# A hybrid decoder layer on one core: scratch rows padded from 34 to 36, and weight loads moved from SyncE's queue to GpSimd's

## The chip, the cores and the metric

The kernel runs on one core of one Trainium2 chip. The metric is device time in microseconds (us) of one execution. Before the change three runs took 1558.58, 1556.44 and 1551.87 us; their median is 1556.44.

Engines are named as in the profile: PE is TensorE (its weight loads are PEld), DVE is VectorE, ACT is ScalarE, POOL is GpSimd, SP is SyncE. L144 is line 144 of the kernel before. Every engine works through its own instructions in the order in which they stand; semaphores tie the engines together. A transfer is issued from one engine's stream, here nearly always from SP.

## The reference

One layer, float32, 528 rows (16 learned rows and 512 frames), width 1024:

```python
h = h + 0.5 * swiglu(rmsnorm(h, norm_ffn1), ffn1_w_in, ffn1_w_out)
u = rmsnorm(h, norm_mix) * valid
P = u @ w_in                       # attention q|k|v, rwkv r|k|v and three loras, two gates
att = sliding_window_attention(rope(q), rope(k), v, sinks)
rw  = token_shift_lerp(rw, rwkv_mu)
rwo = rwkv7_time_mix(...)          # S = S*w + (S a) b' + v k' per step, y = S r
merged = sigmoid(g_att) * (att @ w_attn_branch) + sigmoid(g_rwkv) * (rwo @ w_rwkv_branch)
h = h + merged @ w_out
h = h + 0.5 * swiglu(rmsnorm(h, norm_ffn2), ffn2_w_in, ffn2_w_out)
return rmsnorm(h, norm_final)
```

The time mixing has 16 heads of 64 channels; its state recurrence runs over the rows, one after another.

## The kernel before

Activations lie transposed, channels on the 128 partitions. Three stretches follow each other: the first feed-forward, the mixer, and the output projection with the second feed-forward.

**Weights.** Every dense product takes its weights in tiles of 128 x 512 float32 (256 KB). `load_w` (L135) loads one into a buffer `raw` from SP's queue (L143), ACT rounds it to float32r, `whi` (L144), and DVE takes the rest, `wlo` (L145). `products` (L153) then issues three matmuls per 128 x 128 block (L155 to L157: hi by hi, hi by lo, lo by hi). There are 3 buffers of `raw` and 4 each of `whi` and `wlo` (`WBUFS`), used in turn: a load has to wait until the tile three before it is split, and a split until PE has used the tile four before it.

**The mixer** (`mixer`, L353) is made of generators, one per stage, that a planner interleaves by a table of start times and spans (`PLAN`, `SHIFT`, `LATE`; `run`, L1020); the tile framework's scheduler then fixes each engine's order from its own priorities. The projections, attention (`attend`), gates and the two branch products fill PE around the recurrence.

The recurrence is cut into 8 chunks of 64 rows and a leading part of 16, and the 16 heads into 8 pairs. For pair j the stages are a1 (projections, decay), p (chunk matrices), i (inverse), b (the serial pass over chunks) and t (normalisation, gate). Stage i needs the inverse of unit triangular matrices. For each of the pair's two heads and each chunk it is done by blocks of 32 x 32, through DRAM:

- stage p stores the diagonal blocks into a scratch tensor `Ls` of 34 rows of 32 x 32 (L824, L825): per head 9 upper blocks (8 chunks and the leading part) and 8 lower ones;
- stage i loads `Ls` three times, one copy per column group, to 3 x 34 = 102 partitions of `LT` (L865), and start values to `X` (L866);
- 31 steps of two DVE operations each substitute (L870, `xtmp<-LT,X`; L872, `X<-X,xtmp`);
- three stores bring `X` to a second scratch tensor `Xs` (L876), each 34 rows of 11 pieces of 128 bytes, and four loads bring the blocks from there into `xt` in 32-row transfers (L881, L882);
- `assemble` (L888) adds the off-diagonal block (L894 to L911).

Stage b begins with `pn<-W,g` (L928) and needs `xt` for the first time in `pn<-zy,xt` (L936); DVE and ACT return its result as `W` (L937, L938), PE multiplies again (L941, `py<-W,g`), DVE forms the next `W` (L945, L947).

**POOL** has no transfers. In the mixer it clears buffers: `tm` (L436), `tsx` (L697, L698), `g` (L773), `kbt` (L779), `g1e` and `g1o` (L785), `W` (L833), `LT` (L878). In the feed-forwards it multiplies `sg` (L285).

Of the kernel before, what the change touches and what calls it, by code (L numbers as in the profile page):

```python
# [8 lines left out]
F32 = mybir.dt.float32  # L9
# [4 lines left out]
OP = mybir.AluOpType  # L14
# [94 lines left out]
def hybrid_layer(ctx: ExitStack, tc: tile.TileContext, a, phases="all"):  # L109
    nc = tc.nc  # L110
# [21 lines left out]
    def half(ap):  # L132
        return ap.rearrange("p (h t) -> p h t", h=2)

    def load_w(src, n, M=P, eng=None, pool=None):  # L135

        if pool:
            hi, lo = (pool.tile([P, KW, P], F32R, name=x)[:, :n, :M] for x in ("whi", "wlo"))
        else:
            hi = wp.tile([P, KW, P], F32R, name="whi", bufs=WBUFS[1])[:, :n, :M]  # L140
            lo = wp.tile([P, KW, P], F32R, name="wlo", bufs=WBUFS[2])[:, :n, :M]
        raw = wp.tile([P, KW, P], F32, name="raw", bufs=WBUFS[0])[:, :n, :M]
        nc.sync.dma_start(out=raw, in_=src)  # L143
        nc.scalar.copy(out=hi, in_=raw)  # L144
        (eng or nc.vector).tensor_tensor(out=lo, in0=raw, in1=hi.bitcast(F32), op=OP.subtract)  # L145
        return hi, lo
# [175 lines left out]
    def rsqrt(pool, x, n, eps, cap=3e38, tag="n", scale=1.0):  # L322


        y = pool.tile([P, 16], F32, name=tag + "y")[:, :n]
        t = pool.tile([P, 16], F32, name=tag + "t")[:, :n]
        if eps:
            xs = pool.tile([P, 16], F32, name=tag + "x")[:, :n]
            nc.vector.tensor_scalar(out=xs, in0=x, scalar1=eps, scalar2=None, op0=OP.add)
            x = xs  # L330
        nc.vector.tensor_scalar(out=y.bitcast(I32), in0=x.bitcast(I32), scalar1=-0.5, scalar2=1597463007.0, op0=OP.mult, op1=OP.add)
        for c in (-3.0, -12.0, -768.0):
            nc.vector.tensor_mul(out=t, in0=y, in1=x)  # L333
            nc.vector.tensor_mul(out=t, in0=t, in1=y)  # L334
            nc.vector.scalar_tensor_tensor(out=y, in0=t, scalar=c, in1=y, op0=OP.add, op1=OP.mult)  # L335
        nc.vector.tensor_scalar(out=y, in0=y, scalar1=-scale / 8192, scalar2=cap, op0=OP.mult, op1=OP.min)
        return y
# [15 lines left out]
    def mixer(nm):  # L353
        uh, ul, rstd = nm.sh, nm.sl, nm.rstd
        un.close()
        es = ctx.enter_context(ExitStack())
        ring = es.enter_context(tc.tile_pool(name="mx_r", bufs=2))
        cp = es.enter_context(tc.tile_pool(name="mx_c", bufs=1))
        tp = es.enter_context(tc.tile_pool(name="mx_t", bufs=1))
        sp = es.enter_context(tc.tile_pool(name="mx_s", bufs=2))  # L360
        ap = es.enter_context(tc.tile_pool(name="mx_a", bufs=2))
        ps = es.enter_context(tc.tile_pool(name="mx_ps", bufs=2, space=PSUM))
        dsc = es.enter_context(tc.tile_pool(name="mx_d", bufs=2, space=bass.MemoryType.DRAM))

        def bank(tag):
            if tag in SMALL:
                return small[:, SMALL[tag]]
            return ps.tile([P, 512], F32, name="p" + tag, tag=tag, bufs=BANKS[tag])
# [294 lines left out]
        def pause(n):  # L663
            for _ in range(PAUSE[n]):
                yield

        def chunks(x):
            return x.rearrange("p (c t) -> p c t", t=CH)
# [99 lines left out]
        def stage_p(j, G):  # L768
# [32 lines left out]
            def masked(dst, src, q):  # L801
                m = tri[slice(0, P) if dst.shape[0] == P else LO, q, :]
                if len(dst.shape) == 3:
                    m = m.unsqueeze(1).to_broadcast(list(dst.shape))
                nc.vector.tensor_mul(out=dst, in0=src, in1=m)

            G.Ls = dsc.tile([34, 32, 32], F32, name="Ls")
            for h, U, Vr in ((0, LO, HI), (1, HI, LO)):
                g1, Z, Y = G.g1[h], U, Vr
                pt = bank("s")  # L810
                nc.tensor.matmul(pt[:, 0:P], KBT[:, 0, :], G.g0[:, h, :], start=True, stop=True)
                masked(G.g2[U, 0, :], pt[U, Z], 0)
                masked(G.g0[Vr, h, Z], pt[Vr, Z], 0)
                for c0 in (1, 5):
                    pt = bank("s")
                    for i in range(4):
                        nc.tensor.matmul(pt[:, P * i:P * i + P], KBT[:, c0 + i, :], g1[:, c0 - 1 + i, :], start=True, stop=True)
                    pv = pt.rearrange("p (c t) -> p c t", c=4)
                    masked(G.g2[U, c0:c0 + 4, :], pv[U, :, Z], 0)
                    masked(g1[Vr, c0 - 1:c0 + 3, Z], pv[Vr, :, Z], 0)  # L820
                    masked(g3[:, c0 - 1:c0 + 3, 1 + h, :], pv[:, :, Y], 1)
                    yield
                u = 64 * h
                nc.sync.dma_start(out=G.Ls[17 * h:17 * h + 9].rearrange("c s t -> s c t"), in_=G.g2[u:u + 32, :, 0:32])  # L824
                nc.sync.dma_start(out=G.Ls[17 * h + 9:17 * h + 17].rearrange("c s t -> s c t"), in_=G.g2[u + 32:u + 64, 1:, 32:64])  # L825
            yield
            pb = bank("s")
            nc.tensor.matmul(pb, C("bones"), rkk, start=True, stop=True)
# [27 lines left out]

        def stage_i(j, G):

            Xs = dsc.tile([34, 33, 32], F32, name="Xs")
            G.LT = sp.tile([P, 32, 32], F32, name="LT", bufs=1)  # L860
            LT = G.LT[:102]
            X = sp.tile([102, 11, 32], F32, name="X", bufs=1)
            tmp = sp.tile([102, 11, 32], F32, name="xtmp", bufs=1)
            for q in range(3):
                nc.sync.dma_start(out=LT[34 * q:34 * q + 34], in_=G.Ls)  # L865
            nc.sync.dma_start(out=X, in_=a["xinit"])  # L866
            yield
            for c in range(31):
                n, w = c // 3 + 1, 31 - c
                nc.vector.tensor_tensor(out=tmp[:, :n, :w], in0=LT[:, c:c + 1, c + 1:32].to_broadcast([102, n, w]),  # L870
                                        in1=X[:, :n, c:c + 1].to_broadcast([102, n, w]), op=OP.mult)
                nc.vector.tensor_add(out=X[:, :n, c + 1:32], in0=X[:, :n, c + 1:32], in1=tmp[:, :n, :w])  # L872
                if c % 8 == 7:
                    yield
            for q in range(3):
                nc.sync.dma_start(out=Xs[:, q:33:3, :], in_=X[34 * q:34 * q + 34])  # L876
            G.xt = XT[j % 2]
            nc.gpsimd.memset(G.LT[:, :24, :], 0.0)  # L878
            for h in range(2):
                u, m = 64 * h, 17 * h  # L880
                nc.sync.dma_start(out=G.xt[u:u + 32, :, u:u + 32], in_=Xs[m:m + 9, 0:32, :].rearrange("c s t -> s c t"))  # L881
                nc.sync.dma_start(out=G.xt[u + 32:u + 64, 1:, u + 32:u + 64],  # L882
                                  in_=Xs[m + 9:m + 17, 0:32, :].rearrange("c s t -> s c t"))
            yield
            yield from pause("inv")
            yield from assemble(G)

        def assemble(G):  # L888


            x11, w1 = G.LT[:, :16].rearrange("p (c h) x -> p c h x", h=2), G.LT[:, 16:24]
            for h in range(2):
# [61 lines left out]
        def stage_t(j, G):  # L954
# [4 lines left out]
            spread = lambda x: x.unsqueeze(2).to_broadcast([P, 8, CH])  # L959
            nc.vector.tensor_reduce(out=s1, in_=yg, op=OP.add, axis=AX.X)  # L960
            nc.vector.tensor_scalar(out=s1, in0=s1, scalar1=-1.0 / CH, scalar2=None, op0=OP.mult)
# [3 lines left out]
            nc.scalar.activation(out=sq, in_=ys, func=AF.Square)  # L965
            nc.vector.tensor_reduce(out=s2, in_=chunks(sq), op=OP.add, axis=AX.X)
            rv = rsqrt(sp, s2, 8, CH * GN_EPS, tag="g", scale=8.0)
# [83 lines left out]
        G = [Ctx() for _ in range(NJ)]  # L1051
# [27 lines left out]
        add("rwkv_branch", 0, rwkv_branch(), last, move, g[0])  # L1079
        run(tasks)  # L1080
        assert next(att, None) is None and next(gate, None) is None
        es.close()

    nc.scalar.dma_start(out=vec, in_=a["vec"])
    with ExitStack() as es:
        hp = es.enter_context(tc.tile_pool(name="hp", bufs=1))
        h = hp.tile([P, KD, NT], F32, name="h")
# [30 lines left out]
    with ExitStack() as es:  # L1118
        hp = es.enter_context(tc.tile_pool(name="hp3", bufs=1))
        up2 = es.enter_context(tc.tile_pool(name="up2", bufs=1))  # L1120
        h = hp.tile([P, KD, SEQ], F32, name="h")
# [25 lines left out]
def constants():  # L1147
    c = np.zeros((P, NCON), np.float32)

    def put(n, x):  # L1150
        c[:x.shape[0], CON[n]:CON[n] + x.shape[1]] = x
    put("ident", np.eye(P, dtype=np.float32))
    i = np.arange(P)[:, None] % CH
    jj = np.arange(192)[None, :]
    win = np.where((jj > i) & (jj <= 128 + i), 0.0, 8 * NEG).astype(np.float32)
    z = np.zeros((P, NMETA), np.float32)
    put("am", np.concatenate([win, z], 1))
    b = (np.arange(P)[:, None] // CH == np.arange(P)[None, :] // CH).astype(np.float32)
    put("bones", b)
    x = np.zeros((102, 11, 32), np.float32)  # L1160
    for gcol in range(3):
        for ii in range(11):
            if 3 * ii + gcol < 32:
                x[34 * gcol:34 * gcol + 34, ii, 3 * ii + gcol] = 1
    return c, x


# [61 lines left out]
```

## Time and profile before

The profiled execution took 1557.82 us; the span from its first to its last instruction is 1556.1 us.

| engine | busy in the span, us | share |
|---|---|---|
| PE | 1500.3 | 96% |
| DVE | 900.1 | 58% |
| ACT | 652.9 | 42% |
| POOL | 93.6 | 6% |

| transfers | |
|---|---|
| issued | nearly all from SP (137568 of 137838 packets on its queue) |
| moved | 163.23 MB, mean 105 GB/s |
| weight loads in the mixer | 133 after the norm (`win` 99, `wgd` 2, `wa` 16, `wr` 16) |

Busy shares are means over unlike stretches. Views by stretch, the waits of each engine (who waited for whom, total, times, longest) and the timeline say more. A matmul's end is modelled, so PE counts as busy even where it runs at half clock; the granted clock has a column of its own. A wait is shown with the work that ended last before it was over.

### The profile page before, as it was taken

How to read it: one execution, taken by the hardware profiler on the slowest of the kernel's cores; microseconds unless marked ns; L12 is line 12 of the kernel's file. 1: busy time of each engine (PE TensorE's matmuls, PEld its weight loads, DVE VectorE, ACT ScalarE, POOL GpSimd, SP SyncE). 2: the span in 40 equal slices, each digit the busy share in tenths (PEclk: the TensorE clock that was granted, in tenths of full speed). 3: DMA queues.
4: the chain of work that ended last, by engine and by line, in shares of the span. 5: the costliest groups of instructions: out<-in, count | busy, mean ns of one | idle time of the engine just before them, and what ended most of it. 6: DMA issues, size and time to landing. Idle time of an engine off the chain costs nothing. (4 is left out here: it accounts for less than half of the span.)

```text
span 1556.1 us, 25641 instructions
## 1 busy us (share of the span) xinstructions
PE 1500.3 (96%) x9365; PEld 1325.2 (85%) x9365; DVE 900.1 (58%) x2471; ACT 652.9 (42%) x1468; POOL 93.6 (6%) x153
## 2 busy tenths in 40 slices
PE   9999999999999999998999999999999999999997
PEld 9999999999887888887878887677777888888886
DVE  6334334344764886887978888675655444443334
ACT  5333333233442457465664754635343333332231
POOL 0111111000100000000000000000000111110000
PEclk9999999999999999999989999999999999999998
DMA  5333333344243333323332232555633333333332
GB/s 165 89 93 91 89 93 88 110 120 116 78 121 96 112 84 89 81 81 104 99 98 76 82 101 85 153 183 173 221 95 89 95 95 96 97 97 91 95 97 79
DMA packets 137838, 163.23 MB, mean 105 GB/s; under 512 B 56960, under 2 KB 68288, under 8 KB 137712
## 3 DMA queue, kind: packets, MB, share of 16 engines
q1 hardware_dynamic: 137568, 161.54, 35.4%
q8 instruction: 73, 1.20, 0.3%
q14 instruction: 53, 0.43, 0.1%
q10 hardware_dynamic: 144, 0.06, 0.0%
HBM read 140.03 MB, written 21.52 MB: 104 GB/s over the span
## 5 line engine op out<-in xcount | busy, mean ns | idle before, releaser
L144 ACT CAST whi<-raw 128x512 fp32r<-128x512 f32 (+1 forms) x426 | 258.8, 611 | 576.6 <-PE dn L156 446.5
L145 DVE TENSOR_TENSOR wlo<-raw,whi 128x512 fp32r<-128x512 f32 (+1 forms) x426 | 287.9, 679 | 304.1 <-ACT whi L144 300.0
L155 PE MATMUL dn<-uh,whi 128*128 128x264 f32 (+1 forms) x1320 | 426.8, 323 | 1.9 <-DVE tgt L657 0.9
L156 PE MATMUL dn<-ul,whi 128*128 128x264 f32 (+1 forms) x1320 | 427.3, 324 | 0.3 <-DVE ul L203 0.3
L157 PE MATMUL dn<-uh,wlo 128*128 128x264 f32 (+1 forms) x1320 | 425.0, 322 | 0.0
L155 PEld LDWEIGHTS dn<-uh,whi 128*128 128x128 f32 x1320 | 247.8, 188 | 23.9 <-ACT whi L144 3.2
L157 PEld LDWEIGHTS dn<-uh,wlo 128*128 128x128 f32 x1320 | 248.4, 188 | 19.9
L156 PEld LDWEIGHTS dn<-ul,whi 128*128 128x128 f32 x1320 | 248.4, 188 | 19.0 <-DVE ul L203 0.5
L155 PE MATMUL pdn<-uh,whi 128*128 128x264 f32 (+3 forms) x656 | 229.0, 350 | 4.6 <-ACT whi L144 2.5
L157 PE MATMUL pdn<-uh,wlo 128*128 128x264 f32 (+3 forms) x656 | 224.3, 343 | 3.7 <-DVE wlo L145 3.6
L156 PE MATMUL pdn<-ul,whi 128*128 128x264 f32 (+3 forms) x656 | 224.5, 343 | 0.9 <-DVE ul L253 0.8
L155 PEld LDWEIGHTS pdn<-uh,whi 128*128 128x128 f32 x656 | 127.1, 194 | 17.0 <-ACT whi L144 4.2
L157 PEld LDWEIGHTS pdn<-uh,wlo 128*128 128x128 f32 x656 | 127.0, 194 | 11.4 <-DVE wlo L145 5.0
L156 PEld LDWEIGHTS pdn<-ul,whi 128*128 128x128 f32 x656 | 126.7, 193 | 7.7 <-DVE ul L253 1.7
L155 PE MATMUL dn<-mh,whi 128*128 128x264 f32 (+2 forms) x350 | 110.7, 316 | 0.0
L156 PE MATMUL dn<-ml,whi 128*128 128x264 f32 (+2 forms) x350 | 110.6, 316 | 0.0
L157 PE MATMUL dn<-mh,wlo 128*128 128x264 f32 (+2 forms) x350 | 110.5, 316 | 0.0
L285 POOL TENSOR_TENSOR sg<-sg,rstd 128x528 f32<-128x528 f32 (+1 forms) x44 | 58.0, 1319 | 595.8 <-ACT sg L284 428.9
L286 DVE TENSOR_TENSOR m<-sg,dn 128x528 f32<-128x528 f32 (+1 forms) x44 | 30.6, 696 | 70.9 <-PE dn L157 67.6
L155 PEld LDWEIGHTS dn<-mh,whi 128*128 128x128 f32 x350 | 66.1, 189 | 4.4
L156 PEld LDWEIGHTS dn<-ml,whi 128*128 128x128 f32 x350 | 66.1, 189 | 4.3
L157 PEld LDWEIGHTS dn<-mh,wlo 128*128 128x128 f32 x350 | 66.0, 189 | 4.3
(395 smaller groups left out, 2058.2 us busy)
## 6 DMA issues: line engine op xcount, KB each, us to landing
raw<-win SPq DMA_DIRECT2D x104, 256.0 KB
raw<-w1in SPq DMA_DIRECT2D x88, 256.0 KB
raw<-w2in SPq DMA_DIRECT2D x88, 256.0 KB
raw<-w1out SPq DMA_DIRECT2D x40, 256.0 KB
raw<-w2out SPq DMA_DIRECT2D x40, 256.0 KB
gD<-tgt SPq DMA_DIRECT2D x24, 256.0 KB
raw<-wa SPq DMA_DIRECT2D x16, 256.0 KB
tgt<-gD SPq DMA_DIRECT2D x16, 256.0 KB
```

The source lines that it names most:

```text
L144: nc.scalar.copy(out=hi, in_=raw)
L145: (eng or nc.vector).tensor_tensor(out=lo, in0=raw, in1=hi.bitcast(F32), op=OP.subtract)
L155: nc.tensor.matmul(o, hi, xh[k][:, c], start=(k == 0), stop=False)
L156: nc.tensor.matmul(o, hi, xl[k][:, c], start=False, stop=False)
L157: nc.tensor.matmul(o, lo, xh[k][:, c], start=False, stop=last)
L285: nc.gpsimd.tensor_mul(out=sg, in0=sg, in1=nm.rstd[:, :n])
L286: nc.vector.tensor_mul(out=vw(m), in0=vw(sg), in1=vu)
```

## The change

Two edits.

1. The scratch tensors `Ls` and `Xs` get 36 rows in place of 34, 18 per head, and `X`, `xtmp` and `LT` 3 x 36 = 108 partitions in place of 102. The lower blocks' store now takes all 9 parts, the leading one too, so that each head has 9 + 9 rows; the load of the lower blocks skips that one. The 31 substitution steps are the same, on 108 partitions.
2. `load_w` issues from `queue["w"]`, which is SP's queue in the feed-forwards and the output projection, and POOL's from the mixer's start to its end. The copies to `whi` and `wlo` stay on ACT and DVE.

```diff
+    queue = {"w": nc.sync}
+
     def load_w(src, n, M=P, eng=None, pool=None):
...
-        nc.sync.dma_start(out=raw, in_=src)
+        queue["w"].dma_start(out=raw, in_=src)
...
         es = ctx.enter_context(ExitStack())
+        queue["w"] = nc.gpsimd
         ring = es.enter_context(tc.tile_pool(name="mx_r", bufs=2))
...
-            G.Ls = dsc.tile([34, 32, 32], F32, name="Ls")
+            G.Ls = dsc.tile([36, 32, 32], F32, name="Ls")
...
-                nc.sync.dma_start(out=G.Ls[17 * h:17 * h + 9].rearrange("c s t -> s c t"), in_=G.g2[u:u + 32, :, 0:32])
-                nc.sync.dma_start(out=G.Ls[17 * h + 9:17 * h + 17].rearrange("c s t -> s c t"), in_=G.g2[u + 32:u + 64, 1:, 32:64])
+                nc.sync.dma_start(out=G.Ls[18 * h:18 * h + 9].rearrange("c s t -> s c t"), in_=G.g2[u:u + 32, :, 0:32])
+                nc.sync.dma_start(out=G.Ls[18 * h + 9:18 * h + 18].rearrange("c s t -> s c t"), in_=G.g2[u + 32:u + 64, :, 32:64])
...
             for q in range(3):
-                nc.sync.dma_start(out=LT[34 * q:34 * q + 34], in_=G.Ls)
+                nc.sync.dma_start(out=LT[36 * q:36 * q + 36], in_=G.Ls)
...
             for q in range(3):
-                nc.sync.dma_start(out=Xs[:, q:33:3, :], in_=X[34 * q:34 * q + 34])
+                nc.sync.dma_start(out=Xs[:, q:33:3, :], in_=X[36 * q:36 * q + 36])
...
-                u, m = 64 * h, 17 * h
+                u, m = 64 * h, 18 * h
...
-                                  in_=Xs[m + 9:m + 17, 0:32, :].rearrange("c s t -> s c t"))
+                                  in_=Xs[m + 10:m + 18, 0:32, :].rearrange("c s t -> s c t"))
...
+        queue["w"] = nc.sync
         es.close()
```

The scheduler lays out every engine's order anew. In the changed kernel line numbers are 2 to 5 higher (L143 becomes L145, L876 becomes L880, L936 becomes L940).

SP around the last pair's three stores of `X` and the four loads of `xt`, before:

```order
L1014 DMA pT<-rD 128x512
L643 DMA gD<-tgt 128x512
L143 DMA raw<-wa 128x512
L876 DMA Xs<-X 374x1x32 x3
L643 DMA gD<-tgt 128x512
L637 DMA tgt<-gD 128x512
L143 DMA raw<-wa 128x512
L881 DMA xt_4609<-Xs 32x9x32
```

And in the changed kernel:

```order
L1018 DMA pT<-rD 128x512
L984 DMA tgs<-bD 128x512
L880 DMA Xs<-X 396x1x32 x3
L1018 DMA pT<-rD 128x512 x2
L646 DMA gD<-tgt 128x512
L885 DMA xt_4609<-Xs 32x9x32
```

The weight tiles (`raw<-wa`) are gone from SP; other transfers of 256 KB still stand between the stores and the loads.

POOL around the clearing of `g` for the fourth pair (`g_8031`), before:

```order
L436 MEMSET tm 128x1 x2
L785 MEMSET g1e 64x1024
L785 MEMSET g1o 64x1024
L833 MEMSET W 128x128
L878 MEMSET LT 128x768
L773 MEMSET g_8031 128x256
L436 MEMSET tm 128x1 x2
```

And in the changed kernel:

```order
L439 MEMSET tm 128x1
L145 DMA raw<-win 128x512 x2
L439 MEMSET tm 128x1
L788 MEMSET g1e 64x1024
L788 MEMSET g1o 64x1024
L837 MEMSET W 128x128
L882 MEMSET LT 128x768
L145 DMA raw<-win 128x512
L776 MEMSET g_8031 128x256
L145 DMA raw<-win 128x512 x3
L439 MEMSET tm 128x1
```

The memsets keep nearly their order, and the loads stand between them, singly or up to some ten in a row.

PE at the last pair's first use of `xt`, before:

```order
L155 MATMUL pdn<-uh,whi 128x512
L156 MATMUL pdn<-ul,whi 128x512
L157 MATMUL pdn<-uh,wlo 128x512
L936 MATMUL pn<-zy,xt_4609 128x128
L155 MATMUL pdn<-uh,whi 128x512
L898 MATMUL pt<-LT,gg_11398 128x128 x4
```

And in the changed kernel:

```order
L157 MATMUL pdn<-uh,whi 128x512
L158 MATMUL pdn<-ul,whi 128x512
L159 MATMUL pdn<-uh,wlo 128x512
L940 MATMUL pn<-zy,xt_4609 128x128
L902 MATMUL pt<-LT,gg_11398 128x128 x4
```

Both stand behind dense products of 512 columns. Before, this matmul comes 102 rows after the pair's first W product (`pn<-W,g_11394`), in the changed kernel 54 rows after it.

More of the change, by code (lines that the diff above doesn't have):

```diff
@@ L857, in stage_i @@
         def stage_i(j, G):
-            Xs = dsc.tile([34, 33, 32], F32, name="Xs")
+            Xs = dsc.tile([36, 33, 32], F32, name="Xs")
             G.LT = sp.tile([P, 32, 32], F32, name="LT", bufs=1)
-            LT = G.LT[:102]
-            X = sp.tile([102, 11, 32], F32, name="X", bufs=1)
-            tmp = sp.tile([102, 11, 32], F32, name="xtmp", bufs=1)
+            LT = G.LT[:108]
+            X = sp.tile([108, 11, 32], F32, name="X", bufs=1)
+            tmp = sp.tile([108, 11, 32], F32, name="xtmp", bufs=1)
             for q in range(3):
-                nc.sync.dma_start(out=LT[34 * q:34 * q + 34], in_=G.Ls)
+                nc.sync.dma_start(out=LT[36 * q:36 * q + 36], in_=G.Ls)
             nc.sync.dma_start(out=X, in_=a["xinit"])
@@ L869, in stage_i @@
                 n, w = c // 3 + 1, 31 - c
-                nc.vector.tensor_tensor(out=tmp[:, :n, :w], in0=LT[:, c:c + 1, c + 1:32].to_broadcast([102, n, w]),
-                                        in1=X[:, :n, c:c + 1].to_broadcast([102, n, w]), op=OP.mult)
+                nc.vector.tensor_tensor(out=tmp[:, :n, :w], in0=LT[:, c:c + 1, c + 1:32].to_broadcast([108, n, w]),
+                                        in1=X[:, :n, c:c + 1].to_broadcast([108, n, w]), op=OP.mult)
                 nc.vector.tensor_add(out=X[:, :n, c + 1:32], in0=X[:, :n, c + 1:32], in1=tmp[:, :n, :w])
@@ L1159, in constants @@
     put("bones", b)
-    x = np.zeros((102, 11, 32), np.float32)
+    x = np.zeros((108, 11, 32), np.float32)
     for gcol in range(3):
@@ L1163, in constants @@
             if 3 * ii + gcol < 32:
-                x[34 * gcol:34 * gcol + 34, ii, 3 * ii + gcol] = 1
+                x[36 * gcol:36 * gcol + 36, ii, 3 * ii + gcol] = 1
     return c, x
```

## The prediction

> **What bounds the kernel now.** I read the table of stages first. Its columns are the stretch and its length in us, then the busy time (and the instructions) of PE, PEld, DVE, ACT and POOL, the granted TensorE clock, the DMA share and GB/s.
>
> ```profile
> 0.00:382.00 382.00, 380.31 (x3082) 378.18 (x3083) 162.15 (x252) 132.72 (x215) 30.00 (x28) 1.00 0.36 106
> 382.00:1114.00 732.00, 689.72 (x4340) 593.13 (x4339) 547.33 (x1897) 380.12 (x1026) 34.98 (x103) 0.97 0.37 109
> 1114.00:1556.00 442.00, 430.29 (x1947) 353.84 (x1945) 190.62 (x324) 140.03 (x228) 28.59 (x22) 0.99 0.33 98
> ```
>
> The change acts only in the middle stretch, the mixer (the first weight load that it moves is at 382 us, the last at 1113). TensorE sets the end there too, but it leaves 732.0 - 689.7 = 42.3 us idle and its clock averages 0.97. DVE is busy for 547 of 732 us, POOL for 35. So the ceiling of any gain is the 42 us and the lost clock. The waits of PE in that stretch (total, times, longest) say who owns the idle time:
>
> ```profile
> PE py L941 <- DVE W L937: 5.4, 6, 2.2
> PE pn L928 <- DVE W L947: 5.2, 3, 2.7
> PE pn L936 <- DMA xt<-Xs: 4.7, 4, 2.8
> PE pdn L157 <- DVE wlo L145: 3.6, 3, 2.2
> PE ps L811 <- DVE kbt L794: 2.8, 1, 2.8
> PE pdn L155 <- ACT whi L144: 2.5, 4, 1.1
> ```
>
> The first two are the recurrence, which the change does not touch. The third is the inverse coming back from DRAM. The fourth and sixth are weight tiles that are not split yet, 6.1 us in all. The fifth will turn out to be a transfer as well.
>
> **The padded rows: what they remove.** One pair, the last one, followed through SP, DVE and PE (start, length, instruction; the bracket is idle time and its releaser):
>
> ```profile
> 1039.00 0.17 DVE L872 TENSOR_TENSOR X<-X,xtmp 102x11 f32<-102x11 f32 x1
> ...
> 1039.20 4.70 SPq L876 DMA_DIRECT2D Xs<-X  x3
> 1044.00 2.04 SPq L643 DMA_DIRECT2D gD<-tgt  x1
> ...
> 1048.04 0.33 SPq L881 DMA_DIRECT2D xt<-Xs  x1
> ...
> 1049.41 0.46 SPq L882 DMA_DIRECT2D xt<-Xs  x1
> ...
> 1050.96 0.46 PE L936 MATMUL pn<-zy,xt 128*128 128x128 f32 x2 [2.79 <-DMA xt<-Xs]
> ```
>
> The substitution ends at 1039.17. Its three stores need 4.70 us to issue, and their bytes are there at 1048.04, when the loads that wait for them go out: 8.9 us. Those loads move 2 x 32 x (9 + 8) = 1088 pieces of 128 bytes in 32-row transfers, nearly as many as the stores (3 x 374 = 1122), and PE has them 1050.96 - 1048.04 = 2.9 us after the first is issued. The view of the DMA engines for the first pair's store (583.0 to 589.0 us in 40 slices, tenths busy, then GB/s) says why:
>
> ```profile
> DMA  0000111111111111121222212222211221222212
> GB/s 5 0 0 13 27 27 27 26 27 27 27 27 27 27 26 21 23 22 20 22 22 22 22 20 21 22 22 21 22 20 21 23 22 20 22 22 22 22 20 21
> ```
>
> For over five microseconds one to two tenths of the 16 engines run, about two of them, at 20 to 27 GB/s, and nothing else on SP's queue moves beside them. A 34-row transfer uses about two engines. The first pair's substitution also waits for its input, three 34-row loads:
>
> ```profile
> 531.94 0.91 SPq L865 DMA_DIRECT2D LT<-Ls  x3
> ...
> 543.96 0.19 DVE L870 TENSOR_TENSOR xtmp<-LT,X 102x31 f32<-102x31 f32 x1 [2.57 <-DMA LT<-Ls]
> ...
> 545.02 0.46 PE L811 MATMUL ps<-g,kbt 128*128 128x128 f32 x2 [2.81 <-DVE kbt L794]
> ```
>
> DVE, in order, stands 2.57 us for a load issued 12 us earlier, and PE stands 2.81 us for a product queued behind it. Each of these two stalls costs a second time, in granted clock (the third figure from the right):
>
> ```profile
> 545.00:553.00 8.00, 7.97 (x41) 7.70 (x42) 6.50 (x34) 4.55 (x17) 0.10 (x1) 0.59 0.11 37
> ...
> 1051.00:1058.00 7.00, 6.28 (x22) 5.40 (x23) 2.72 (x7) 2.54 (x8) 0.00 (x0) 0.55 0.66 219
> ```
>
> 8 x 0.41 = 3.3 us and 7 x 0.45 = 3.2 us of PE's time are lost.
>
> The cost of a 36-row transfer is in no row. Bounds: as now (no gain), or as the 32-row loads, 2.9 us instead of 8.9. I take the second end: 36 is the nearest to 32 in rows and pieces. That is 6 us off each store, and more than the 2.57 off the load. The extra work is small: X grows from 374 to 396 pieces, and the DVE steps run over partitions, 108 in place of 102, at the same length.
>
> The Trainium skill, "DMA: Bandwidth & Descriptors", section "Why a DMA increments its semaphore by 16 and not by 1", has a rule for this: a transfer is spread over the largest number up to 16 that divides its slowest dimension, so 34 rows go to 2 engines and 36 to 12. The two tenths above agree for 34; for 36 no run here shows it yet. By that rule the store would take a sixth of its time, some 1 us as an estimate, and the sum below would be the same, since 2.9 us already clears the waits.
>
> Terms. (a) The stall at 545 goes with its clock loss: -2.8 - 3.3 = -6.1. (b) Three smaller waits for xt: 4.7 - 2.8 = -1.9. (c) The stall at 1051 with its clock loss is 2.8 + 3.2 = 6.0, but the new order puts that pair's first use of xt closer behind the pair's start (54 rows of PE after its first W product; 102 before), which uses up part of what the faster store gives. I take half: -3.0. Bounds for (a) to (c): 0 and -14.0.
>
> **The weights on POOL's queue.** 133 loads leave SP (99 + 2 + 16 + 16). What they do now (issue time min/median/max in ns, first and last start; then what the split of a tile waited for, us and times):
>
> ```profile
> L143 SPq DMA_DIRECT2D raw<-win x99: 327/351/846, 387.4 to 985.8; - x99
> L143 SPq DMA_DIRECT2D raw<-wa x16: 332/390/1312, 996.4 to 1052.5; - x16
> L143 SPq DMA_DIRECT2D raw<-wr x16: 327/332/430, 1057.7 to 1113.4; - x16
> L143 SPq DMA_DIRECT2D raw<-wgd x2: 374/378/381, 382.1 to 385.0; - x2
> ...
>   PE pdn L156: 40.6, 37
>   DMA raw<-win: 25.7, 12
> ...
>   DMA raw<-wr: 3.9, 1
>   DMA raw<-wa: 2.6, 3
> ```
>
> An issue takes SP 0.35 us. The ACT cast of a tile waits 37 times for PE to release a buffer (the load was early) and 16 times for the load, 32.2 us in all; of these PE sees the 6.1 us above. Part of the lateness is SP's order, for a load stands behind transfers that wait:
>
> ```profile
> SPq L613 <- ACT ao L611: 28.3, 11, 5.2
> SPq L737 <- ACT rw L735: 27.6, 7, 11.2
> SPq L998 <- DVE tys L996: 24.1, 4, 11.7
> ```
>
> Away from SP a load no longer waits for ao, rw or tys, nor behind two busy engines. (d) I take a third of the 6.1 us: -2.0; bounds 0 and -6.1. On POOL it instead stands behind memsets, which wait too (longest groups of POOL; busy, mean ns of one | idle before):
>
> ```profile
> L785 POOL MEMSET g1e<- 64x1024 f32 x8 | 7.6, 952 | 53.5 <-PE pn L928 53.4
> L436 POOL MEMSET tm<- 128x1 f32 (+1 forms) x27 | 2.6, 98 | 321.4 <-DVE tr L446 177.6 <-DVE tk L446 63.8 <-DVE tv L446 49.4
> ```
>
> Most of that idle time is POOL arriving early with nothing else to do, and the scheduler has put the loads between memsets of about the same age. Behind a load that waits for its raw buffer now stand the memsets, for which DVE and PE wait; the tm memset is 98 ns of work and its wait was DVE's own.
>
> What POOL needs to issue a load is in no row. Bounds: SP's 0.35 us below; above, POOL's own largest operation:
>
> ```profile
> L285 POOL TENSOR_TENSOR sg<-sg,rstd 128x528 f32<-128x528 f32 (+1 forms) x44 | 58.0, 1319 | 595.8 <-ACT sg L284 428.9
> ```
>
> I take the upper, 1.3 us, the one whole-tile operation of POOL that the trace shows. 133 x 1.3 = 173 us of POOL's 732: not a bound. A load lands 1.3 - 0.35 = 1.0 us later. (e) Early loads hide that behind PE's buffers; the 16 late ones do not: 16 us more for ACT, of which PE sees the present share, 6.1 / 32.2 = 0.19: +3.0. Without that cover all 16 us would reach PE. Bounds 0 and +16.
>
> A rule that speaks against the move: the Trainium skill, "SBUF — State Buffer", section "Who interferes with whom", says that a load issued from GpSimd has its descriptors written by GpSimd's cores, which certain DVE operations lock out, and "A bandwidth-pool intuition that's wrong (but worth ruling out)" on the same page gives some 620 ns alone and 3100 ns beside such an operation. No run here shows it; rival 4 works out in rows what it would do.
>
> Sum: -6.1 - 1.9 - 3.0 - 2.0 + 3.0 = -10.0 us. The profiled execution took 1557.82 us (span 1556.1 and 1.7 around it), so 1547.8; the median of the runs shown, 1556.44, is 1.4 lower, which gives **1546.4 us**. By itself this case runs from 1540 to 1552 (a sum of -16 to -4: (c) whole or not at all, (d) and (e) at half or twice what is taken).
>
> **Rivals.** (1) *More comes free.* With SP empty of weights every small transfer of the chain goes out when it is ready, and all of (a) to (d) fall with no cost on POOL: -14.0 - 6.1 = -20.1, thus 1536. For: SP's waits of 80 us in the three rows above. Against: PE sees little of them.
> (2) *Nothing on balance.* The chain is shorter, but DVE, at 547 of 732 us and in order, hands the time on to the recurrence (10.6 us in the first two waits of PE), or the 36-row transfers still use two engines, so that the change does not do what it says: 1554 to 1559.
> (3) *Slower: head of line on POOL.* A load stands behind the g1e memset, which waits for PE to finish with a pair two back (53.4 us over the eight). From the point where that delay exceeds what three raw buffers hold, PE runs dry and the clock drops with it. A stall like the one at 545 costs 2.8 + 3.3 = 6.1 us; in four of the eight pairs that is +24, less the 9 of the padding: +15, thus 1571. For: the memset's waits are long, and POOL cannot reorder. Against: casts find their load early 37 times to 16.
> (4) *Each load held up on POOL by DVE.* DVE is busy three quarters of the stretch; if an issue takes POOL 3 us, still under the 732 / 133 = 5.5 us that it may, the 16 late loads land 2.65 us later, 42 us on ACT, of which PE sees 0.19: +8.0 in place of +3.0, so 1551.4. This is the rule of the SBUF page above.
>
> **How the numbers follow.** What a measurement of this kernel can tell from no change is about 0.5%, 7.8 us: faster is under 1548.7, slower over 1564.2. Forecast 0.38 (0.30 of it faster, 0.08 the same); rival 1 0.17, all faster; rival 2 0.17 (0.13 the same, 0.04 slower); rival 3 0.20 (0.19 slower, 0.01 the same); rival 4 0.08 (0.03 faster, 0.05 the same). Together faster 0.50, same 0.27, slower 0.23. The range takes in rival 1 with some 6 us of the remaining idle time, and rival 3 to its middle: 1530 to 1570.
>
> **What would show it.** Right: the DMA share in a store rises well above two tenths, SP issues the three stores in under 3 us, the waits of PE for xt and for kbt go and the half-clock stretches behind them; waits of ACT for raw stay near 32 us. Wrong: POOL's loads start late behind L785 or L436, PE's waits for whi and wlo grow past 15 us, or the waits for W grow by what xt lost. A mean clock under 0.97 in the mixer would say that new stalls took the place of the old.

## The result and the profile after

The changed kernel takes 1527.62 us (median of four runs, 1526.39 to 1531.18) against 1555.19 us before (four runs: the three above and one of 1553.94): a ratio of 0.983, 95% interval [0.980, 0.985], 27.6 us faster. The forecast was 1546.4 and its range ended at 1530: the sign was right, the size was not, and the sum of the terms (-10.0) held little more than a third of the gain.

The stages of the changed kernel, in the columns of the prediction's first table (busy time by engine, granted clock, DMA share, GB/s):

```profile
0.00:382.00 382.00, 380.17 (x3082) 378.12 (x3083) 162.35 (x252) 132.82 (x215) 29.99 (x28) 1.00 0.36 106
382.00:1087.00 705.00, 678.63 (x4338) 582.57 (x4337) 550.48 (x1899) 381.18 (x1026) 106.74 (x236) 0.98 0.39 115
1087.00:1529.00 442.00, 430.58 (x1948) 354.04 (x1947) 190.19 (x322) 140.43 (x228) 28.61 (x22) 0.99 0.33 96
```

All of it is in the mixer: 705 us in place of 732, the other two stretches are as they were. PE's idle time there fell from 42.3 to 705.0 - 678.6 = 26.4 us; the other 11 us are busy time, which shrank as the granted clock rose from 0.97 to 0.98. POOL's 72 us more are the issuing of loads. The longest waits of PE in that stretch (total, times, longest):

```profile
PE pn L940 <- ACT zy L933: 3.0, 6, 0.8
PE pdn L157 <- DVE tgt L645: 2.5, 1, 2.5
PE pdn L159 <- DVE wlo L147: 2.5, 2, 2.2
PE pt L912 <- ACT LT L906: 2.0, 4, 0.8
```

The waits for `xt` (4.7) and `kbt` (2.8) are gone, and so are most of those for `W` (1.9 us left of 10.6), which the prediction took to lie outside the change. The transfers themselves became faster. SP's timeline at the first pair's store, before and then after (start, length of the issue):

```profile
582.15 4.28 SPq L876 DMA_DIRECT2D Xs<-X  x3
...
590.54 0.33 SPq L881 DMA_DIRECT2D xt<-Xs  x1
```

```profile
579.57 2.58 SPq L880 DMA_DIRECT2D Xs<-X  x3
...
584.32 0.33 SPq L885 DMA_DIRECT2D xt<-Xs  x1
```

From the store's issue to the first load of `xt` it is 4.8 us in place of 8.4. The view of the DMA engines over that store and the loads behind it (580 to 586 us, tenths busy) shows up to nine tenths where it was one or two. Part of it is POOL's: 46% of the 16 engines' time is SP's queue, 23% the weight loads.

```profile
DMA  9998620486130698899968994768998505646445
```

The weight loads on POOL (issue min/median/max in ns), their time to landing, and the waits of ACT's casts for them:

```profile
L145 POOL DMA_DIRECT2D raw<-win x99: 539/539/557, 387.7 to 932.7; - x99
...
DMA to landing us min/median/max: 2.5/3.2/5.7
```

```profile
ACT whi L146 <- PE pdn L158: 88.6, 67, 4.5
...
ACT whi L146 <- DMA raw<-win: 5.7, 3, 3.4
```

An issue costs POOL 0.54 us, the same with DVE busy for 550 of 705 us, and the casts wait 5.7 us for loads in place of 32.2. So both edits do what they say. Which of them carries the gain is a question for the experiments.

### The profile page after: what moved, and what is told of

Same layout as the page of the kernel before. It is cut to its first block, busy times and chain, and to the rows that moved or that the text cites. A ratio compares the mean times of both kernels' runs of the same rounds, so it can differ in the third digit from the quotient of the medians.

```text
span 1529.5 us, 25746 instructions
## 1 busy us (share of the span) xinstructions
PE 1489.4 (97%) x9365; PEld 1314.7 (86%) x9365; DVE 903.0 (59%) x2471; ACT 654.4 (43%) x1468; POOL 165.3 (11%) x286
## 5 line engine op out<-in xcount | busy, mean ns | idle before, releaser
L145 POOL DMA_DIRECT2D raw<-win x99 | 53.4, 539 | 313.7 <-DVE wlo L147 127.4
```

The costliest lines, as they stand in the source:

```text
L145: queue["w"].dma_start(out=raw, in_=src)
```

## The pairs in a row

The traces of all kernels agree in one thing that the prediction did not look at: the distance from one pair to the next. The loads of `LT` (three per pair; issue times in ns, first and last start), before and then after:

```profile
L865 SPq DMA_DIRECT2D LT<-Ls x24: 251/272/324, 531.9 to 989.2; - x24
```

```profile
L869 SPq DMA_DIRECT2D LT<-Ls x24: 306/358/758, 532.6 to 962.6; - x24
```

The first pair starts at the same time; the eighth starts 26.6 us earlier. The seven distances between pairs shrank from 457.3 / 7 = 65.3 to 430.0 / 7 = 61.4 us, 27.3 us together, as much as the gain. One tile keeps the inverse of a pair from overlapping with that of the next: `LT` has one buffer, and `assemble` keeps its last operand in it. In the kernel before, SP's own waits between 420 and 1000 us have this row:

```profile
SPq L865 <- PE pt L908: 10.8, 5, 3.5
```

Five of the seven following loads wait for the last product of `assemble`. So load, 31 steps, store, `xt`, `assemble` and the next load form a loop, and what a transfer loses in it can be lost in every pair, whether PE shows a wait for it or not. How much of it is lost, the runs below have to show. In the table below the four pieces are means over seven pairs, from the start times in the timeline (first `LT` load, first step, first `Xs` store, first `xt` load, next `LT` load); the distance is worked out as above.

| kernel | time, us | distance | load to step | steps | store to xt | xt to next load |
|---|---|---|---|---|---|---|
| before | 1555.2 | 65.3 | 11.3 | 36.6 | 8.5 | 8.8 |
| after | 1527.6 | 61.4 | 8.9 | 35.3 | 5.1 | 12.0 |
| e1 padding alone | 1523.0 | 61.3 | 9.5 | 34.8 | 4.8 | 12.2 |
| e2 queue alone | 1592.9 | 70.1 | 12.2 | 36.9 | 9.0 | 11.9 |
| e3 38 rows, POOL | 1605.8 | 71.3 | 13.1 | 36.7 | 9.9 | 11.6 |
| e4 loads later on POOL | 1533.2 | 62.3 | 8.7 | 36.5 | 5.2 | 11.7 |
| e5 38 rows, SP | 1585.0 | 68.2 | 12.5 | 35.6 | 9.3 | 10.8 |
| e6 40 rows, SP | 1527.9 | 61.5 | 9.2 | 34.1 | 4.9 | 13.2 |
| e7 only the load wide | 1550.0 | 63.3 | 9.8 | 35.4 | 8.8 | 9.2 |
| e8 only the store wide | 1579.0 | 69.2 | 15.1 | 38.0 | 6.3 | 9.6 |
| e9 before, LT free earlier | 1551.5 | 64.3 | 11.8 | 35.3 | 8.4 | 8.8 |
| e10 e1, LT free earlier | 1522.0 | 59.8 | 9.6 | 35.1 | 4.6 | 10.4 |
| e11 before, LT held longer | 1584.1 | 70.3 | 11.2 | 36.5 | 8.4 | 14.0 |
| e12 queue alone, on ACT | 1582.5 | 68.3 | 11.9 | 36.8 | 9.2 | 10.3 |

A straight line through the 14 rows, time against seven distances, has a slope of 1.03 us per us and misses none by more than about 9 us. That by itself is arithmetic more than a cause, since the seven distances are part of the time. It says where the time goes; what makes a distance long is what the runs had to show.

## The experiments

The scheduler lays out every engine anew for each kernel, so single results carry some scatter of order: e1 and e6, two kernels with wide transfers (spread over many DMA engines) and their loads on SP, lie 5 us apart, and e8 below shows that an order can cost far more. All are compared with the kernel before on the same chip.

**One edit at a time (e1, e2).** The first takes the diff of the change with the queue left on SP; the second the queue with 34 rows.

```diff
-        queue["w"] = nc.gpsimd
+        queue["w"] = nc.sync
```

> The padded rows alone; all weights stay on SP's queue. Theory P (the transfers over two engines were nearly the whole cost): 20 us or more below the kernel before, DVE's waits for LT and xt (19 us together before) under 5 us, three Xs stores issued in under 3 us. Theory Q (the in-order queue on SP was the larger part): about the terms (a) to (c) of the prediction, 8 to 12 us below, with ACT's waits for raw still near 30 us.

> The queue alone; 34 rows stay. Theory P: within 5 us of the kernel before, since the stalls at LT and xt remain. Theory Q: 12 to 20 us below, ACT's waits for raw under 10 us, while DVE's waits for LT and xt stay near 19 us. Should both edits alone give their full size, the two add up to the 27.6 us of the change; if they share a cause, they overlap.

The padding alone: 1522.96 us, 0.979 [0.978, 0.981], 32 us faster. The queue alone: 1592.94 us, 1.025 [1.022, 1.028], 38 us slower. The padding is more than the whole gain; the queue edit costs. So the theory that puts the gain on the padding (P) stands, and the one that puts it on the queue (Q) falls. With 36 rows it costs 1527.6 - 1523.0 = 4.7 us, at the edge of what the two intervals tell apart; with 34 rows it costs 38. The edits do not add. In the two profiles as much lies behind the last pair's `LT` load: from there to the end of the mixer it is 119.7 us at a clock of 1.00 with the padding alone, 124.4 at 0.96 with both edits.

DVE's waits for the two transfers, before and with the queue alone:

```profile
DVE xtmp L870 <- DMA LT<-Ls: 10.8, 5, 2.8
DVE LT L894 <- DMA xt<-Xs: 8.2, 7, 1.7
```

```profile
DVE xtmp L873 <- DMA LT<-Ls: 28.8, 7, 5.4
DVE LT L897 <- DMA xt<-Xs: 23.4, 8, 6.5
```

and PE's waits with the queue alone:

```profile
PE pn L931 <- DVE W L950: 14.0, 4, 4.4
PE pn L939 <- DMA xt<-Xs: 13.5, 6, 5.7
PE py L944 <- DVE W L940: 10.4, 5, 4.8
```

DVE stands 52 us in order where it stood 19, and what is queued behind it is the recurrence's `W`. Weight tiles are not what is late here: ACT's waits for `raw` fell, from 32.2 to 20.6 us.

**The number of rows (e3, e5, e6).** 38 rows with the loads on POOL; 38 and 40 rows with the loads on SP. The added rows are filled by one small extra store per pair, and nothing uses them.

```diff
-            G.Ls = dsc.tile([36, 32, 32], F32, name="Ls")
+            G.Ls = dsc.tile([38, 32, 32], F32, name="Ls")
...
+            nc.sync.dma_start(out=G.Ls[36:38].rearrange("c s t -> s c t"), in_=G.g2[0:32, 0:2, 0:32])
```

> The changed kernel with 38 rows in place of 36 (19 x 2; two rows more are filled by one small transfer per pair and used by nothing). If what counts is the number of engines, 38 rows go back to two: the store shows one to two tenths of DMA share for some 6 us again, the three issues take over 4 us, and the time comes out near that of the queue edit alone. If padding helps in another way (row pitch, size), it stays within 4 us of the changed kernel.

> 38 scratch rows, all loads on SP; one small extra transfer per pair fills the two extra rows, which nothing uses. Theory E (the padding pays because 36 rows are spread over many engines): 38 rows are back on two engines, so the three Xs stores take 9 to 11 us until xt can be loaded, PE's waits for xt return and the time is 1553 to 1568, near the 1555 of before. It also repeats the measurement of the queue edit on two-engine rows with another order of instructions: against the 1605.8 of 38 rows with the loads on POOL. Theory O (the padding pays because the scheduler happened to find a better order of instructions, whatever the engines): no relation to the count of engines; the time stays within 10 us of the 1523.0 of 36 rows as likely as not.

> 40 scratch rows, all loads on SP; one small extra transfer per pair fills the four extra rows, which nothing uses. Theory E: the transfer is spread wide again (8 engines if the count is the largest one that divides the rows), so Xs to xt takes 4.5 to 5.5 us and the time is 1522 to 1532, close to the 1523.0 of 36 rows although there are more rows than in the slow 38. Theory O: anything between 1520 and 1570.

Measured: 1605.81 us (1.033 [1.030, 1.035]) for 38 rows on POOL, 1584.97 (1.019 [1.017, 1.022]) for 38 on SP, 1527.88 (0.983 [0.981, 0.984]) for 40 on SP. More rows than 36 are fast at 40 and slow at 38, and store to `xt` goes with it: 4.8, 4.9 us against 9.3, 9.9. That is the rule of the Trainium skill, "DMA: Bandwidth & Descriptors", section "Why a DMA increments its semaphore by 16 and not by 1" (the largest number up to 16 that divides the rows: 36 gives 12, 40 gives 8, 38 and 34 give 2). The times agree with it, and 12 engines are no faster here than 8. That the good order came by chance (theory O) would need 40 rows to be fast and 38 slow twice by luck, and more: the five kernels in which load and store are both wide take 1522 to 1533 us, the nine others 1550 and above. It falls as the cause, though a share of each size can be the order's. But 38 rows on SP cost 17 us more than the top of what was expected. Their `LT` load and store are each about 1 us longer than with 34 rows, as 4 rows more on two engines would make them, and the way back to the next load 2 us. The queue edit costs here again, 1605.8 - 1585.0 = 21 us, in another order of instructions.

**Load or store (e7, e8).** The padding alone, with each of the three stores, or each of the three loads, issued as 34 and 2 rows, so that this one is back on two engines.

```diff
-                nc.sync.dma_start(out=Xs[:, q:33:3, :], in_=X[36 * q:36 * q + 36])
+                nc.sync.dma_start(out=Xs[0:34, q:33:3, :], in_=X[36 * q:36 * q + 34])
+                nc.sync.dma_start(out=Xs[34:36, q:33:3, :], in_=X[36 * q + 34:36 * q + 36])
```

> As the padding alone, but each Xs store is issued as 34 rows and 2 rows, so that the store runs on two engines again while the LT load keeps 36 rows. Theory E with the store as the larger part (about 4 us per pair on the chain against 2 to 3 for the load): 1540 to 1550; the wait of PE for xt returns (4 us or more), the stall at kbt does not. If the load is the larger part: under 1535. Theory O: no relation.

> As the padding alone, but each LT load is issued as 34 rows and 2 rows, so that the load runs on two engines again while the Xs store keeps 36 rows. Theory E with the store as the larger part: 1528 to 1538; DVE's waits for LT return (about 8 to 11 us), PE's waits for xt stay away. If the load is the larger part: over 1540. The two halves of the gain should add to about 32 us, within 6. Theory O: no relation.

With a narrow store: 1549.99 us, 0.996 [0.995, 0.998], that is 27 us of the 32 lost again. SP's timeline of one pair:

```profile
707.95 0.69 SPq L880 DMA_DIRECT2D Xs<-X  x1
708.69 1.34 SPq L881 DMA_DIRECT2D Xs<-X  x1
...
716.62 0.33 SPq L886 DMA_DIRECT2D xt<-Xs  x1
```

The store takes 8.7 us again, 4.0 more than with 36 rows in one piece. Seven times that is 28, but the sum does not come about in that way: the way back to the next load took up 3.0 of the 4.0, the steps and the load cost 0.9 more, and the distance grew by 2.0, 14 us in seven. Most of the rest, 10.7 us, lies behind the last pair's load, where the clock is 0.93 in place of 1.00 (130.4 us to the end of the mixer, 119.7 with the padding alone). PE showed no wait for `xt`, where 4 us or more were expected, and DVE one of 2.9 us in all. So a slow transfer costs here without standing in PE's list of waits.

With a narrow load: 1578.95 us, 1.015 [1.013, 1.018], far above the 1528 to 1538 that was expected. The halves add to 27 + 56 = 83 us, not to 32. The reason is seen in DVE: it has no wait for `LT` at all, since the first step stands behind other work, 15.1 us after the load and not 9.5. The order had put it there. So e8 does not measure a two-engine load; it measures what an order with a longer loop costs: 5.6 us more there, 3.2 in the steps and 1.5 in the store, less 2.6 on the way back, leave 7.7 per pair, and seven times that is 54 of the 56 us.

**The loop itself (e9, e10, e11).** No transfer of the loop is changed. In e9 and e10 `w1`, the last thing in `LT`, goes to `xtmp`, so that the next load has to wait for L898 only; e9 starts from the kernel before, e10 from the padding alone. In e11, on the kernel before, `w1` is stored and read back from POOL's queue, so that `LT` is held longer; nothing uses the copy.

```diff
-            x11, w1 = G.LT[:, :16].rearrange("p (c h) x -> p c h x", h=2), G.LT[:, 16:24]
+            x11, w1 = G.LT[:, :16].rearrange("p (c h) x -> p c h x", h=2), G.xtmp[:, :8]
```

```diff
+            wD = dsc.tile([P, 8, 32], F32, name="wD")
+            nc.gpsimd.dma_start(out=wD, in_=w1)
...
+            nc.gpsimd.dma_start(out=w1, in_=wD)
```

> The kernel before (34 rows, loads on SP) with one buffer moved: w1, the last thing that assemble keeps in LT, goes to xtmp, so that the next pair's LT load waits for the product at L898 and no longer for L908, about 2.4 us earlier; no transfer changes. Theory L (the pairs follow each other in a closed loop through the single LT buffer: load, 31 steps, store, xt, assemble, next load; what the loop loses, the mixer loses seven times): 2 us off each of seven pairs, 1555 - 14 = 1541, range 1535 to 1549. Theory W (a slow transfer costs only what PE visibly waits for it): the waits of PE for xt and kbt stay, and the time is within 5 us of 1555.

> The padding alone (36 rows, loads on SP) with the same buffer moved. Theory L: with the faster transfers the loop has 3 to 5 us to spare in most pairs (xt load to next LT load 12 us, where 7 to 8 is the least seen), so 2.4 us more brings little: 1523 - 0 to 6 = 1517 to 1523. If the loop still binds as it did before: 1523 - 14 = 1509. Theory W: 1523 within 5.

> The kernel before with LT held longer: after assemble has written w1 it is stored to a scratch tensor and read back, both from POOL's queue, and nothing uses the copy; the next LT load has to wait for it, some 3 us longer than for L908. Theory L: 3 us on each of five to seven pairs, +15 to +21: 1570 to 1576. Theory W: PE does not wait for these transfers, so 1555 within 5.

Held longer: 1584.05 us, 1.019 [1.016, 1.022], 30 us slower. SP's wait for `LT` and the distance between pairs:

```profile
SPq L865 <- DMA LT<-wD: 10.5, 4, 5.9
```

```profile
L865 SPq DMA_DIRECT2D LT<-Ls x24: 252/272/315, 531.0 to 1022.8; - x24
```

The delay turned out as 14.0 - 8.8 = 5.2 us per pair, not 3, and the distance grew by 70.3 - 65.3 = 5.0: seven times 5.0 is 35, of which 30 are seen. It came nearly one for one from a delay for which PE has no wait; the other pieces of the loop stayed within 0.1 us. Theory W, by which a slow transfer costs only PE's own waits, falls on this run.

Freed earlier: 1551.50 us, 0.999 [0.998, 1.001]: no change that can be told, where 14 us were expected and theory W had forecast none. The edit did what it should, for the load now waits for the earlier product, and less:

```profile
SPq L866 <- PE pt L900: 2.0, 2, 1.2
```

and three of the seven ways back shrank to 4.5 to 5.1 us. But two grew, from 7.5 and 9.4 to 12.5 and 16.8 us, and a third, at 13.7 before, came down only to 10.1: there the next load stood behind its own pair's `Ls` store (in one, the store was issued at 848.9 and the load at 853.1). So the loop through `LT` is one of two limits of nearly the same length; the other is the stage that feeds it. Theory L holds for what is added to the loop, and not for what is taken away at that one place. That leaves a question: the padding too only takes away, and it gained. In its trace the feeding stage is faster as well, the last `Ls` stores of the fifth to the seventh pair 62.1 and 61.6 us apart, against 68.8 and 67.2 in e9. Which of its effects does this, DVE standing less for `LT` and `xt` (19.0 us in all before, 21.6 in e9, 0.4 with the padding) or another, no run separates. On the padded kernel the same edit gave 1521.96 us against 1522.96, as expected no difference, though the distance fell to 59.8. With the padding alone PE is close to its limit: it is busy for 675.8 of 700 us at a clock of 0.99:

```profile
382.00:1082.00 700.00, 675.76 (x4346) 578.37 (x4345) 547.08 (x1898) 379.86 (x1025) 35.11 (x103) 0.99 0.39 115
```

**The queue (e4, e12).** In e4, the changed kernel with two memsets of 128 x 512 on POOL ahead of each of the mixer's loads, nothing else is done; e12 is the queue edit alone, with ACT's queue in place of POOL's.

> The changed kernel with two clears of the 128x512 raw tile on POOL ahead of each weight load of the mixer, some 1 us more on POOL per load. It tests term (e) of the prediction, that a load issued 1 us later costs PE 3 us in all. If (e) holds: 2 to 5 us over the changed kernel. If the loads have more slack on their own queue: within 2 us. If POOL's queue is tight: 10 us or more.

> The queue edit alone with 34 rows, but the mixer's weight loads issued from ACT's queue in place of POOL's. Theory R (any second queue for the weights makes the two-engine transfers later or lets the scheduler place their users too early): DVE's waits for LT and xt stay near the 52 us of the POOL variant, time 1580 to 1600; ACT's own issue time adds to it. Theory S (it is POOL's way of issuing): DVE's waits fall back to some 19 us and the time is 1550 to 1565.

With the memsets POOL is busy for 243 us of the mixer in place of 107, and the time is 1533.19, 0.986 [0.984, 0.988]: 5.6 us more, just above the 2 to 5 that term (e) stood for. Of the 136 us more that POOL had to do ahead of its loads, the rest was covered. The queue edit on ACT: 1582.54 us, 1.019 [1.017, 1.021], 28 us slower than before. DVE's waits:

```profile
DVE xtmp L873 <- DMA LT<-Ls: 27.7, 7, 7.0
DVE LT L897 <- DMA xt<-Xs: 13.3, 6, 5.1
```

41 us, nearer to POOL's 52 than to the 19 of one queue. So most of the 38 us comes with a second queue of whichever engine, though ACT's own issuing, 0.33 us a load, is in its 28. How it does that is not settled. In e2 the load and the store are together 1.4 us longer per pair than before; that is 10 us of the 38. The rest of the distance (steps +0.3, way back +3.1) may come from the order that the scheduler chose for DVE and SP, which it could not be made to keep while the queue changed.

## Why the prediction was wrong, point by point

**Terms (a) to (c), the padding: the step that failed.** They gave -11.0, with a bound of -14.0; the padding alone measured -32. The price of a 36-row transfer was taken too high, not too low: 6 us off each store was said and 3.7 came, more than 2.57 off the load was said and 1.8 came, and the store did not come down to some 1 us, a sixth, but to 4.8, of which 2.6 are its issue. What failed is the step from there to the time. The prediction put the savings against PE's visible waits for `xt` and `kbt` and their clock, and stopped where those waits were used up ("2.9 us already clears the waits").

The traces show where the gain was in its place. With the padding alone the two places that the sum priced came near it: the distance from the first pair to the second, which holds the stall at 545, shrank from 65.4 to 59.8 us (term (a): -6.1), and the stretch from the last pair's load to the mixer's end, which holds the one at 1051, from 124.8 to 119.7 (term (c): -3.0). The other six distances, for which the sum had at most the 1.9 of (b), gave 22.4. In the changed kernel the two priced places gave nearly nothing (64.8 and 124.4 us) and the six distances 26.8. The wait of 2.8 for `kbt` went there too, but the half-clock stretch that was priced with it stayed, at 0.57 in place of 0.59:

```profile
545.00:553.00 8.00, 8.00 (x44) 8.00 (x43) 6.38 (x33) 3.66 (x10) 0.00 (x0) 0.57 0.10 33
```

So the saving should have been counted per turn of a loop that eight pairs pass through one after another: 3.7 + 1.8 per pair, seven times, is 38 us. That is an upper estimate. With the padding alone the steps shrank by 1.8 as well and the way back grew by 3.4, which leaves 4.0 per pair, 28 us in the seven distances, of the 32 measured; and e9 shows that a saving in this loop need not come through at all. The row that points to the loop, SP's wait of L865 for PE's L908, was in the trace of before and was not read.

**The bound.** "TensorE sets the end there too" was right only in part. The ceiling drawn from it, 42 us of idle time and the lost clock, held. But PE idles in many small pieces under other names: `W` at L937 and L947, 10.6 us "which the change does not touch", went from PE's longest waits. That DVE no longer stood for `LT` and `xt` ahead of them is one possible reason; but in e9, where it stood as long as before, these waits fell to 4.0 us too, so the reason stays open. And the sum priced the lost clock at two places only: with the padding alone PE's idle time fell from 42.3 to 24.2 us and its busy time by 14.1, at a clock of 0.99.

**Terms (d) and (e), the queue.** Together +1.0 was taken; with 36 rows +4.7 was measured, which is inside the bounds. Their parts were off in both directions. POOL's issue takes 0.54 us, not 1.3. ACT's waits for `raw` did not stay near 32 us but fell to 5.7, so the gain of (d) was there for ACT, and PE's waits for `whi` and `wlo` fell from 6.1 to 4.2 us. That the sum of (d) and (e) came out inside its bounds is luck. A cost beyond (e), from the second queue, was not foreseen.

**The rivals.** (1), more comes free, 1536, was the nearest, but by luck, since its reason is refuted: SP empty of weights costs 38 us in e2 and 4.7 with the padding. (2) fell: the time did not go to the recurrence, and 36 rows are not on two engines. (3) fell: POOL's loads stand behind its memsets, but e4, with 136 us more of work ahead of them, lost only 5.6 us. (4) fell: the issue of a `win` load took 539 ns at the median and 557 at most beside a DVE busy for 78% of the stretch (the two `wgd` loads took 762 and 922). So the lock-out of the page "SBUF — State Buffer" of the Trainium skill, section "Who interferes with whom", is not seen here; most of that DVE time is TENSOR_TENSOR operations, so it says little of others.

**What would show it.** The DMA share in the store, the store's issue under 3 us, and the waits for `xt` and `kbt` came out as said, and the mean clock rose to 0.98. Two items did not: ACT's waits for `raw` fell to 5.7 us, and the half-clock stretch at 545 stayed. None of the signs asked about the distance between pairs.

The fastest version here is the padding without the queue edit, 1522.96 us, or the same with `w1` moved, 1521.96; the two cannot be told apart.

## What to carry to other kernels

When a chain of transfers recurs once per block, look for what closes it into a loop (a tile with one buffer, and the queue's wait for its last reader), and price a saving per turn times the turns, as an upper estimate: a second limit close behind the first can take it back, as in e9. PE's list of waits shows only where the delay surfaced last. Count how many DMA engines a transfer's rows divide over before anything else is tuned around it: two rows of padding were worth 32 us, and with two more the time was 62 us longer. Test two edits apart, since one can carry the gain and the other cost part of it.

## What the runs showed that was not expected

A second queue for the weights is no free relief: with two-engine transfers beside it, 28 us (ACT) to 38 us (POOL) slower, although the weights themselves arrived earlier (ACT's waits for `raw` 20.6 in place of 32.2 us). Padding to 38 rows was worse than 34 on the same queue by 29 us, for 12% more rows. And a buffer freed 2.4 us earlier in the loop brought nothing, while one held 5 us longer cost 30: two limits of nearly equal length look like one until one of them is moved.
